# A hybrid decoder step: table load and splits placed behind the last Silu, mixer work dealt anew among ScalarE, VectorE and GpSimd

## The chip, the cores and the metric

The kernel runs on one core of one Trainium2 chip. The metric is the device time of one execution in microseconds; the time of a kernel is the median of its runs.

## The reference, cut to what matters

512 prompt tokens and 8 single-token samples (520 columns in all) pass through one layer of width 1024. The mixer has four mLSTM heads (matrix memory with exponential gates) and four retention heads of width 128; each head's output is normalised and gated. Then come an output projection, cross-attention into 256 memory tokens, a SwiGLU feed-forward of width 2816, and a last norm. Everything is in float32.

```
def layer(x, ...):
    u = rmsnorm(x, g_mix) @ w_in
    qk, conv_new = short_conv(u[..., :2 * M], conv_buf, w_conv, b_conv)      # silu(conv)
    hm, C, n, m = mlstm_scan(mq, mk, mv, ig, lf, C0, n0, m0)                 # 4 heads, chunks of 128
    hm = head_rmsnorm(hm, g_mhead) * jax.nn.sigmoid(mo)
    rq = rope(r[..., :R]...); rk = rope(r[..., R:2 * R]...) * (R_HEAD_DIM ** -0.5)
    hr, S = retention_scan(rq, rk, rv, S0)                                   # 4 heads, chunks of 128
    hr = head_rmsnorm(hr, g_rhead) * jax.nn.silu(rg)
    x = x + jnp.concatenate([hm, hr], axis=-1) @ w_out
    x = x + cross_attn(rmsnorm(x, g_xattn), mk_mem, mv_mem, w_cq, w_co)
    hf = rmsnorm(x, g_ffn)
    x = x + (jax.nn.silu(hf @ w_gate) * (hf @ w_up)) @ w_down
    return x, conv_new, C, n, m, S

def head_rmsnorm(h, g):
    h = h * lax.rsqrt(jnp.mean(h * h, axis=-1, keepdims=True) + EPS)
    return h.reshape(B, T, H * D) * g
```

The outputs are `rmsnorm` of the result with `g_final`, the new memory keys and values, and the new states.

## The kernel before

Activations lie transposed: features on 128 partitions, the 520 columns along the free axis, in halves of 260. A float32 matrix is split into a high part in fp32r and a low remainder, and a product is made of three: high by high, high by low, low by high. A projection of 128 output columns is therefore 8 blocks of depth x 3 products x 2 halves, 48 matmuls (`proj`, `mm_k`). Weights come by DMA on SyncE's queue into `wraw`; `wload` casts them on ScalarE to `whi` and forms the remainder `wlo` on VectorE, or on GpSimd where the weight's index stands in `LO_ON_POOL`. `split` does the same for activations: the cast on ScalarE, the remainder on VectorE (`TT` in the feed-forward, `B` and `A` before).

The stages follow one another: first norm (up to 20 us), mixer (20 to 262), output projection (to 310), cross-attention (to 490), gate and up projections of the feed-forward (to 727), down projection (to 838), last output block and last norm (to 873).

In the mixer TensorE runs one projection after another: `conv_block` (`pcv`) makes q and k of a mLSTM head, `plain_block` (`ppl`) the values, `rope_block` (`prp`) q and k of a retention head, and the gate projections (`pgt`) close the stage. Between them stand the pieces of the head before, as generators that `step()` moves on: `mlstm` and `retention` fetch the samples' state (`Cs`, `Ss`, 128x1024) by a DMA on GpSimd's queue, scale it, transpose keys and values (`token_major`: `vt`, `kw`), make the decayed scores (`E`, `w`), the queries with decay (`qd`), the chunk states (`states`: `St`), the outputs (`weighted`: `hs`) and then `head_norm`. That takes the sum of squares of each of four chunks and the samples into `s5` (128x5, named `hs` in the rows), an inverse root by a seed and three Newton steps in `rsqrt_small` (`hny`, `hnt`), a scaling of `hs` by it, and five transposes `ph` on TensorE. A generator called `gates` runs beside the first head: its scans `m_r` and `b_r` on VectorE yield the decays (`pc`, `cc`, `Gb`, `ws`, `car`, `fib`).

In the feed-forward the first 4 of 22 column blocks are plain; the other 18 are made of 7 products of half matrices (`pfc`, `pfd`, `pfa`, `pfa`, `pfe`, `pfb`, `pfb`), put together in `gu`: L1230 to L1243, where a Silu of the gate half and a product give `FR`. The high and low parts of `FR`, which the down projection reads, are made by `ff_split`. The parts of the first 8 blocks stand in `A`'s place; those of blocks 8 to 21 (`unsplit`) go by `rest_split`: two after each of the last products of the last block, the others behind each second depth step of the down projection. The down projection's first two output blocks run side by side: for 8 blocks of `FR` one weight for each of the two, 96 matmuls, then the next 8 blocks.

The table preload at L1254 fetches the activation table that holds both Ln and Exp. The last output block is made in two parts of columns, of which the second is finished in two quarters: `finish` adds it to `X`, squares, and calls `rsqrt_rows` (Ln, Exp and one Newton step), then multiplies all of `X` into the output and sends it.

The order of instructions on each engine is set by a scheduler that simulates the engines, not by the order of the code; `keep_in_program_order` holds an instruction to its place in the code. Each engine then works through its own list in order, so an instruction that waits holds up all behind it on the same engine.

## Time and profile before

| | us |
|---|---|
| median of 3 runs (875.74 to 878.33) | 876.3 |
| the profiled execution | 874.8 |
| its span in the profile | 873.0 |
| TensorE busy / its weight load | 833.0 (95%) / 816.0 (93%) |
| VectorE busy | 671.6 (77%) |
| ScalarE busy | 406.7 (47%) |
| GpSimd busy | 179.4 (21%) |

PE is TensorE's matmul, PEld its weight load, DVE VectorE, ACT ScalarE, POOL GpSimd. Rows of windows give a stretch of the span (from:to), its length, the busy time of each engine with its count of instructions, TensorE's granted clock as a share of full speed, the busy share of the DMA engines and GB/s. Rows of waits give who waited for whom: the sum in us, how often, and the longest. Rows of the timeline give start and duration in us, engine, line, operation, output and inputs with their sizes, the count of instructions gathered in the row, and in brackets the idle time before it with what released it. Rows of groups give a count, the busy time and the mean in ns of one, then the idle time before them.

### The profile page before, as it was taken

What the parts mean: (1) busy time and instruction counts of PE and PEld (TensorE: products, weight loads), DVE (VectorE), ACT (ScalarE), POOL (GpSimd) and SP (SyncE); (2) the same over time, 40 slices, a digit from 0 to 9 for tenths busy, and PEclk for the clock granted to TensorE, in tenths of its full rate; (3) what the DMA queues carried; (4) which work ended last, traced back from release to release, by engine and by line L of the source; (5) the groups of instructions that cost most, each with busy time, mean ns of one, the idle gap of its engine ahead of it and who ended that gap; (6) DMA issues with size and microseconds to landing.
All of it is one profiled execution on the core that took longest, in us unless ns stands there. A gap on an engine that the chain in (4) does not pass through costs nothing.

```text
span 873.0 us, 17065 instructions
## 1 busy us (share of the span) xinstructions
PE 833.0 (95%) x6707; PEld 816.0 (93%) x6707; DVE 671.6 (77%) x1512; ACT 406.7 (47%) x798; POOL 179.4 (21%) x185
## 2 busy tenths in 40 slices
PE   6989999999999999999999899999999998999992
PEld 5989989999999999889999899999999998999992
DVE  6999999877786777876888899999999996222314
ACT  5545435434546353466442655555455555222324
POOL 5554442222024300415232400000000000000100
PEclk9999999999999999999999999999999999999996
DMA  8333223333345346894764223323334331333302
GB/s 273 99 98 124 88 94 123 124 100 125 103 147 194 114 129 200 266 305 107 241 206 149 73 73 106 111 87 110 98 98 120 117 104 59 105 96 91 107 5 98
DMA packets 32680, 110.56 MB, mean 127 GB/s; under 512 B 4000, under 2 KB 6176, under 8 KB 32344
## 3 DMA queue, kind: packets, MB, share of 16 engines
q1 hardware_dynamic: 27216, 95.80, 35.0%
q0 software_dynamic: 3616, 12.34, 4.1%
q10 hardware_dynamic: 1768, 1.34, 0.5%
q8 instruction: 53, 0.87, 0.4%
q14 instruction: 27, 0.22, 0.1%
HBM read 100.38 MB, written 9.07 MB: 125 GB/s over the span
## 4 chain that ended last, share of the span: by engine, by line
PE 73%; DVE 16%; DMA 4%; ACT 3%; issue 2%; POOL 1%; SPq 0%; DVEq 0%; ACTq 0%; POOLq 0%
PE pfd L1266 13%; PE pfb L1224 6%; PE pfa L1224 6%; PE pcq L223 5%; PE pgt L223 4%; PE pwc L223 4%; PE ppl L223 4%; PE pwo L223 3%; PE pfc L1224 3%; PE pfd L1224 3%; PE prp L223 3%; PE pfe L1224 3%; PE pfu L223 2%; DVE cv L518 2%; DVE wlo L209 2%
## 5 line engine op out<-in xcount | busy, mean ns | idle before, releaser
L208 ACT CAST whi<-wraw 128x1024 fp32r<-128x1024 f32 (+1 forms) x104 | 107.2, 1032 | 174.1 <-PE pfd L1266 66.4
L209 DVE TENSOR_TENSOR wlo<-wraw,whi 128x1024 fp32r<-128x1024 f32 (+1 forms) x85 | 110.0, 1296 | 67.2 <-ACT whi L208 65.2
L302 POOL TENSOR_TENSOR ssq<-ssq,sq 128x520 f32<-128x520 f32 x18 | 28.8, 1601 | 358.6 <-ACT sq L301 353.4
L1266 PE MATMUL pfd<-TT,whi 128*128 128x260 f32 x392 | 62.8, 283 | 0.0
L191 ACT CAST qhi<-wsum 128x512 fp32r<-128x512 f32 x72 | 42.9, 620 | 40.5 <-DVE wsum L1175 26.9
L209 POOL TENSOR_TENSOR wlo<-wraw,whi 128x1024 fp32r<-128x1024 f32 x19 | 45.6, 2398 | 66.2 <-ACT whi L208 61.2
L1224 PE MATMUL pfb<-TT,qhi 128*128 128x260 f32 x288 | 52.8, 283 | 2.4 <-DVE gu L1240 2.4
L1266 PEld LDWEIGHTS pfd<-TT,whi 128*128 128x128 f32 x392 | 53.7, 188 | 0.0
L1224 PE MATMUL pfa<-TT,qhi 128*128 128x260 f32 x288 | 53.1, 282 | 0.0
L192 DVE TENSOR_TENSOR qlo<-wsum,qhi 128x512 fp32r<-128x512 f32 x72 | 48.9, 682 | 0.6 <-ACT qhi L191 0.6
L223 PE MATMUL pwc<-B,whi 128*128 128x260 f32 x256 | 43.7, 287 | 4.2 <-DVE X L291 3.0
L223 PE MATMUL ppl<-A,whi 128*128 128x260 f32 x256 | 46.3, 294 | 0.6 <-DVE up L510 0.6
L1224 PEld LDWEIGHTS pfb<-TT,qhi 128*128 128x128 f32 x288 | 44.4, 188 | 2.6 <-ACT TT L191 2.6
L223 PE MATMUL pcv<-A,whi 128*128 128x260 f32 x256 | 45.3, 293 | 0.4 <-ACT whi L208 0.4
L1224 PEld LDWEIGHTS pfa<-TT,qhi 128*128 128x128 f32 x288 | 44.3, 188 | 0.0
L223 PE MATMUL pgt<-A,whi 128*128 128x260 f32 x256 | 44.0, 287 | 0.0
L223 PE MATMUL prp<-A,whi 128*128 128x260 f32 x256 | 43.8, 287 | 0.0
L223 PE MATMUL pcq<-A,whi 128*128 128x260 f32 x256 | 42.0, 283 | 0.0
L223 PE MATMUL pwo<-B,whi 128*128 128x260 f32 x256 | 41.4, 283 | 0.0
L1224 PE MATMUL pfb<-TT,qlo 128*128 128x260 f32 x144 | 40.7, 283 | 0.0
L223 PEld LDWEIGHTS pwc<-B,whi 128*128 128x128 f32 x256 | 35.8, 188 | 5.3 <-DVE X L291 3.7
L1224 PE MATMUL pfa<-TT,qlo 128*128 128x260 f32 x144 | 40.5, 281 | 0.0
(437 smaller groups left out, 2617.5 us busy)
## 6 DMA issues: line engine op xcount, KB each, us to landing
wraw<-in_weights_dram SPq DMA_DIRECT2D x132, 512.0 KB, 3.7
kv<-in_cache_k_dram SPq DMA_DIRECT2D x16, 512.0 KB, 4.4
kv<-in_cache_v_dram SPq DMA_DIRECT2D x16, 512.0 KB, 4.4
wraw<-in_weights_dram SPq DMA_DIRECT2D x8, 384.0 KB, 3.0
X<-in_x_dram SPq DMA_DIRECT2D x2, 1040.0 KB, 6.2
Cs<-in_state_C_dram POOLq DMA_DIRECT2D x4, 512.0 KB, 4.9
out_dram<-Cs POOLq DMA_DIRECT2D x4, 512.0 KB, 3.2
Ss<-in_state_S_dram POOLq DMA_DIRECT2D x4, 512.0 KB, 3.9
```

Source lines behind the costliest of these rows:

```text
L191: act.copy(hi, src)
L192: dve.tensor_tensor(lo, src, hi.bitcast(F32), ALU.subtract)
L208: act.copy(hi[:, :n], raw[:, :n])
L209: (pool if index in LO_ON_POOL else dve).tensor_tensor(lo[:, :n], raw[:, :n], hi[:, :n].bitcast(F32), ALU.subtract)
L223: pe.matmul(ps[:m, a, :H2], w[:, k, c0 : c0 + m], x[:, s, xk, a * H2 : (a + 1) * H2], start=first and w is hi and s == 0, stop=last and w ...
L302: (dve if ob == KB - 1 else pool).tensor_tensor(ssq, ssq, s, ALU.add)
L518: dve.scalar_tensor_tensor(cv[:, :LO], up[:, j : j + LO], wc(j), cv[:, :LO], ALU.mult, ALU.add)
L1224: pe.matmul(out, w[:, k * P : (k + 1) * P], x[:, k * H2 : (k + 1) * H2], start=k == 0 and w is wh and x is xh, stop=k == 3 and w is wl,)
L1266: pe.matmul(ps[:, a, :H2], w[:, k - k0], ff(s, k, slice(a * H2, (a + 1) * H2)), start=k == 0 and w is hi and s == 0, stop=k == FB - 1 and ...
```

## The change

It has three parts. The table preload is placed behind the last Silu of the feed-forward, by an edge of order instead of a place in the code. The splits of blocks 8 to 21 are placed behind that Silu and behind the last product into `FR` (`read`), and those from block 16 on keep their place in the code. In the mixer: three weights' remainders go from GpSimd to VectorE, as do the gating of k, the last addition of the rope, the `qd` products and the two products that scale the rope's tables; the swap of halves in the rope goes through two copies on ScalarE; the scaling of `Cs` goes from one GpSimd instruction a head to eight on ScalarE, one for each sample; in the head norms the Newton steps and the small products around them go from VectorE to GpSimd, the five scalings from VectorE to ScalarE, and there is one more `yield`.

```diff
-LO_ON_POOL = {2, 4, 11, *range(52, 56), *range(60, 72)}
+LO_ON_POOL = {*range(52, 56), *range(60, 72)}
...
-            act.copy(hi, src)
-            dve.tensor_tensor(lo, src, hi.bitcast(F32), ALU.subtract)
+            return act.copy(hi, src), dve.tensor_tensor(lo, src, hi.bitcast(F32), ALU.subtract)
...
-    def rsqrt_small(pl, v, shape, tag, steps=3):
+    def rsqrt_small(pl, v, shape, tag, steps=3, on_pool=False):
...
-        for _ in range(steps):
+        for _ in range(steps if on_pool else 0):
+            pool.tensor_tensor(t, y, y, ALU.mult)
+            pool.tensor_tensor(t, t, v, ALU.mult)
+            pool.tensor_scalar(t, t, -0.5, 1.5, ALU.mult, ALU.add)
+            pool.tensor_tensor(y, y, t, ALU.mult)
+        for _ in range(0 if on_pool else steps):
...
-            if kb < 4:
-                dve.scalar_tensor_tensor(dst[:, :T], th[:, :T], 1.0, cv[:, :T], ALU.add, ALU.mult)
-            else:
-                pool.tensor_scalar(dst[:, :T], th[:, :T], 1.0, None, ALU.add)
-                pool.tensor_tensor(dst[:, :T], dst[:, :T], cv[:, :T], ALU.mult)
+            dve.scalar_tensor_tensor(dst[:, :T], th[:, :T], 1.0, cv[:, :T], ALU.add, ALU.mult)
...
-            sw = tm("sw")[:, :N]
+            sn, sw = (tm(z)[:, :N] for z in ("sn", "sw"))
+            dve.tensor_tensor(halves(sn), ps[:, :, :H2], halves(sinr), ALU.mult)
             dve.tensor_tensor(halves(dst), ps[:, :, :H2], halves(cosr), ALU.mult)
-            dve.tensor_tensor(halves(sw[:64]), ps[64:, :, :H2], halves(sinr[64:]), ALU.mult)
-            dve.tensor_tensor(halves(sw[64:]), ps[:64, :, :H2], halves(sinr[:64]), ALU.mult)
-            pool.tensor_tensor(dst, dst, sw, ALU.add)
+            act.copy(sw[:64], sn[64:])
+            act.copy(sw[64:], sn[:64])
+            dve.tensor_tensor(dst, dst, sw, ALU.add)
...
             if rho is not None:
-                dve.tensor_tensor(s5, s5, rho, ALU.mult)
-                dve.tensor_tensor(s5, s5, rho, ALU.mult)
-            dve.tensor_scalar(s5, s5, 1.0 / HD, EPS, ALU.mult, ALU.add)
-            f5 = rsqrt_small(sm, s5, [P, 5], "hn")
+                pool.tensor_tensor(s5, s5, rho, ALU.mult)
+                pool.tensor_tensor(s5, s5, rho, ALU.mult)
+            pool.tensor_scalar(s5, s5, 1.0 / HD, EPS, ALU.mult, ALU.add)
+            f5 = rsqrt_small(sm, s5, [P, 5], "hn", on_pool=True)
             if rho is not None:
-                dve.tensor_tensor(f5, f5, rho, ALU.mult)
+                pool.tensor_tensor(f5, f5, rho, ALU.mult)
+            yield
             for j in range(TB):
-                dve.tensor_scalar(hs[:, j, :HD], hs[:, j, :HD], f5[:, j : j + 1], None, ALU.mult)
-            dve.tensor_scalar(hs[:NS, 4, :HD], hs[:NS, 4, :HD], f5[:NS, 4:5], None, ALU.mult)
+                act.activation(hs[:, j, :HD], hs[:, j, :HD], AF.Copy, scale=f5[:, j : j + 1])
+            act.activation(hs[:NS, 4, :HD], hs[:NS, 4, :HD], AF.Copy, scale=f5[:NS, 4:5])
...
-            pool.tensor_tensor(Cs, Cs, fib[:, :, 0, h].unsqueeze(2).broadcast_to([P, NS, HD]), ALU.mult)
+            for b in range(NS):
+                act.activation(Cs[:, b], Cs[:, b], AF.Copy, scale=fib[:, b, 0, h : h + 1])
...
-            pool.tensor_tensor(qd, qd, q[:, P:T].rearrange("p (c t) -> p c t", c=TB - 1), ALU.mult)
+            dve.tensor_tensor(qd, qd, q[:, P:T].rearrange("p (c t) -> p c t", c=TB - 1), ALU.mult)
...
-                pool.tensor_tensor(cosr, cosr, r_bc, ALU.mult)
-                pool.tensor_tensor(sinr, sinr, r_bc, ALU.mult)
+                dve.tensor_tensor(cosr, cosr, r_bc, ALU.mult)
+                dve.tensor_tensor(sinr, sinr, r_bc, ALU.mult)
...
-            ff_split(f, FR[:, f - KB])
+            with tc.issue_after(silu.ins), tc.issue_after(read.ins):
+                both = ff_split(f, FR[:, f - KB])
+            if f >= 2 * KB:
+                for ins in both:
+                    tc.keep_in_program_order(ins)
...
-                act.activation(g2, g2, AF.Silu)
+                silu = act.activation(g2, g2, AF.Silu)
                 to = FR[:, f - KB if f >= KB else f]
-                dve.tensor_tensor(halves(to), gu[:, 0:2], gu[:, 2:4], ALU.mult)
+                read = dve.tensor_tensor(halves(to), gu[:, 0:2], gu[:, 2:4], ALU.mult)
...
-                if j > 3:
-                    rest_split(2)
...
-    tc.keep_in_program_order(act.preload_act_table_set(LOG_EXP))
+    with tc.issue_after(silu.ins):
+        act.preload_act_table_set(LOG_EXP)
```

ScalarE at the end of the feed-forward's last block, before (L1254 is the preload, L1233 and L1241 are Silus, `TT<-FR` are casts of splits, `whi` and `qhi` of weights):

```order
L191 CAST TT<-FR 128x520 x3
L1254 ACT_TABLE_LOAD
L191 CAST TT<-FR 128x520
L191 CAST qhi<-wsum 128x512
L191 CAST TT<-FR 128x520
L208 CAST whi<-wraw 128x1024
L191 CAST TT<-FR 128x520 x3
L1233 ACT_TABLE_LOAD
L1233 ACTIVATE gu<-gu 128x260
L1241 ACTIVATE gu<-gu 128x260
L191 CAST TT<-FR 128x520 x3
L1241 ACTIVATE gu<-gu 128x260
```

The same place of the changed kernel (L1260 is the preload, L1240 and L1248 are Silus):

```order
L191 CAST qhi<-wsum 128x512
L207 CAST whi<-wraw 128x1024
L1240 ACTIVATE gu<-gu 128x260
L1248 ACTIVATE gu<-gu 128x260 x2
L1260 ACT_TABLE_LOAD
L191 CAST TT<-FR 128x520 x8
L207 CAST whi<-wraw 128x1024 x2
L191 CAST TT<-FR 128x520 x4
```

The load stands behind the last Silu now, and the casts of the splits of blocks 8 to 21 behind the load; before, the list had a load ahead of these Silus and a second one for them. Behind this place the list before has six more loads, all at L273 and L275, and the list of the changed kernel none.

VectorE at the same place, before (`gu<-pf..` are the readings of TensorE's products, `TT<-FR,TT` the remainders of splits):

```order
L1238 TENSOR_TENSOR gu<-pfe,gu 128x2x260
L1232 TENSOR_TENSOR gu<-pfd,gu 128x260
L192 TENSOR_TENSOR TT<-FR,TT 128x520 x4
L192 TENSOR_TENSOR qlo<-wsum,qhi 128x512
L1240 TENSOR_TENSOR gu<-pfb,gu 128x520
L1235 TENSOR_TENSOR gu<-pfa,gu 128x260
L192 TENSOR_TENSOR TT<-FR,TT 128x520 x4
L209 TENSOR_TENSOR wlo<-wraw,whi 128x1024
L1236 TENSOR_TENSOR gu<-pfa,gu 128x260
L1243 TENSOR_TENSOR FR<-gu 128x520
```

VectorE there in the changed kernel:

```order
L1239 TENSOR_TENSOR gu<-pfd,gu 128x260
L1245 TENSOR_TENSOR gu<-pfe,gu 128x2x260
L191 TENSOR_TENSOR qlo<-wsum,qhi 128x512
L1242 TENSOR_TENSOR gu<-pfa,gu 128x260
L1247 TENSOR_TENSOR gu<-pfb,gu 128x520
L208 TENSOR_TENSOR wlo<-wraw,whi 128x1024
L1243 TENSOR_TENSOR gu<-pfa,gu 128x260
L1250 TENSOR_TENSOR FR<-gu 128x520
L1245 TENSOR_TENSOR gu<-pfe,gu 128x2x260
L1247 TENSOR_TENSOR gu<-pfb,gu 128x520
L1250 TENSOR_TENSOR FR<-gu 128x520
L191 TENSOR_TENSOR TT<-FR,TT 128x520 x8
```

The two groups of four splits ahead of the readings have gone behind the last product into `FR`.

ScalarE at the first mLSTM head, before (`Ms` is the high part of the samples' k and q, which TensorE's `kq` waits for):

```order
L586 COPY vt_353<-pvt 128x4x128
L521 ACTIVATE th<-cv 128x544
L489 ACTIVATE car<-car 128x16
L491 ACTIVATE ws<-ws 128x16
L516 ACTIVATE cv<-up,vec 128x544
L589 ACTIVATE kw<-pkt,ws 128x128 x4
L191 CAST Ms_351<-kq 8x256
L681 ACTIVATE E<-E,cc 128x128 x4
L688 ACTIVATE qd<-prow,Gb 128x128 x3
L208 CAST whi<-wraw 128x1024
```

ScalarE there in the changed kernel:

```order
L587 COPY vt_353<-pvt 128x4x128
L520 ACTIVATE cv<-up,vec 128x544
L666 ACTIVATE Cs<-Cs,fib 128x128 x8
L493 ACTIVATE car<-car 128x16
L495 ACTIVATE ws<-ws 128x16
L666 ACTIVATE Cs<-Cs,fib 128x128 x8
L191 CAST Ms_351<-kq 8x256
L684 ACTIVATE E<-E,cc 128x128 x4
L691 ACTIVATE qd<-prow,Gb 128x128 x3
L590 ACTIVATE kw<-pkt,ws 128x128 x4
L525 ACTIVATE th<-cv 128x544
L207 CAST whi<-wraw 128x1024
```

Sixteen scalings of states, those of two heads, now stand ahead of `Ms`, `E`, `qd` and `kw`, and `kw`, `th` and the weight cast have gone behind them.

GpSimd between two retention heads, before (L633 is the fill of `s5`, L541 the rope's addition):

```order
L541 TENSOR_TENSOR qr_2194<-qr_2194,sw 128x520
L633 MEMSET hs_2734 128x5
L541 TENSOR_TENSOR kr_2195<-kr_2195,sw 128x520
L751 DMA out_dram<-Ss 128x1024
L729 TENSOR_TENSOR qd<-qr_1872,cst 128x384
L725 DMA Ss<-in_state_S_dram 128x1024
```

GpSimd there in the changed kernel (the last four rows stand three times, one for each Newton step):

```order
L754 DMA out_dram<-Ss 128x1024
L728 DMA Ss<-in_state_S_dram 128x1024
L641 TENSOR_SCALAR hs_2474<-hs_2474 128x5
L262 TENSOR_TENSOR hnt<-hny 128x5
L263 TENSOR_TENSOR hnt<-hnt,hs_2474 128x5
L264 TENSOR_SCALAR hnt<-hnt 128x5
L265 TENSOR_TENSOR hny<-hny,hnt 128x5
```

The long products have gone, and a chain of 13 small instructions stands behind the two DMA issues.

## Rows read from the trace of the kernel before

**Rows 1.** Windows of the whole kernel's core: the mixer in two stretches

```profile
20.00:140.00 120.00, 114.63 (x934) 111.73 (x933) 113.38 (x297) 57.36 (x152) 53.64 (x75) 0.99 0.34 106
140.00:260.00 120.00, 119.64 (x1004) 118.37 (x1003) 97.23 (x304) 56.30 (x144) 26.96 (x26) 1.00 0.37 117
```

**Rows 2.** Waits of TensorE: us in total, times, longest

```profile
PE ph L651 <- DVE hs L645: 2.6, 4, 1.0
...
PE pc L462 <- DVE b_r L444: 1.1, 1, 1.1
```

**Rows 3.** Windows of three short stretches of the mixer

```profile
28.00:44.00 16.00, 16.00 (x137) 15.63 (x136) 15.16 (x40) 8.24 (x14) 10.44 (x22) 1.00 0.41 131
44.00:56.00 12.00, 10.35 (x74) 9.87 (x74) 11.94 (x26) 3.67 (x8) 4.13 (x5) 0.86 0.28 76
64.00:68.00 4.00, 2.58 (x20) 2.25 (x19) 3.94 (x6) 0.32 (x1) 2.22 (x4) 1.00 0.00 0
```

**Rows 4.** Timeline of TensorE at the handover to the down projection: start, duration

```profile
723.52 0.48 PE L1224 MATMUL pfb<-TT,qhi 128*128 128x260 f32 x2 [2.40 <-DVE gu L1240]
...
727.68 0.74 PE L1266 MATMUL pfd<-A,whi 128*128 128x260 f32 x4 [1.05 <-DVE gu L1236]
```

**Rows 5.** Timeline of VectorE at the handover

```profile
719.65 2.52 DVE L192 TENSOR_TENSOR TT<-FR,TT 128x520 fp32r<-128x520 f32 x4
...
722.69 0.69 DVE L1240 TENSOR_TENSOR gu<-pfb,gu 128x520 f32<-128x520 f32 x1
```

**Rows 6.** Timeline of ScalarE at the handover

```profile
726.31 1.14 ACT L191 CAST TT<-FR 128x520 fp32r<-128x520 f32 x2
...
733.51 1.05 ACT L208 CAST whi<-wraw 128x1024 fp32r<-128x1024 f32 x1 [0.38 <-PE pfd L1266]
```

**Rows 7.** Timeline of TensorE: the last matmul of the down projection

```profile
855.19 0.28 PE L1306 MATMUL pfd<-TT,wlo 128*128 128x260 f32 x1
```

**Rows 8.** Timeline of VectorE in the tail

```profile
855.59 2.46 DVE L1294 TENSOR_TENSOR FR<-X,r 128x780 f32<-128x780 f32 x3
857.97 0.48 DVE L1284 TENSOR_TENSOR X<-X,pfd 128x130 f32<-128x130 f32 x2
```

**Rows 9.** Timeline of ScalarE in the tail

```profile
850.65 1.28 ACT L273 ACT_TABLE_LOAD   x1 [2.47 <-PE pn L1288]
...
859.40 1.28 ACT L273 ACT_TABLE_LOAD   x1
...
864.39 1.28 ACT L275 ACT_TABLE_LOAD   x1
865.68 0.31 ACT L275 ACTIVATE nrml<-nrml 128x130 f32<-128x130 f32 x1
```

**Rows 10.** Timeline of VectorE in the first part of the mixer

```profile
25.26 1.78 DVE L276 TENSOR_TENSOR r_bc<-nrml 128x260 f32<-128x260 f32 x1
...
30.60 1.21 DVE L209 TENSOR_TENSOR wlo<-wraw,whi 128x1024 fp32r<-128x1024 f32 x1
...
36.76 2.37 DVE L518 SCALAR_TENSOR_TENSOR cv<-up,vec,cv 128x544 f32<-128x544 f32 x1
...
39.17 0.79 DVE L518 SCALAR_TENSOR_TENSOR cv<-up,vec,cv 128x544 f32<-128x544 f32 x1
```

**Rows 11.** Timeline of GpSimd in the first part of the mixer

```profile
36.16 2.39 POOL L209 TENSOR_TENSOR wlo<-wraw,whi 128x1024 fp32r<-128x1024 f32 x1
...
60.08 4.36 POOL L663 TENSOR_TENSOR Cs<-Cs,fib 128x1024 f32<-128x1024 f32 x2 [2.36 <-DMA Cs<-in_state_C_dram]
...
79.50 0.18 POOL L511 COPY cu<-up 128x3 f32<-128x3 f32 x1 [1.29 <-DVE up L509]
79.64 1.28 POOL L512 COPY cu<-up 128x24 f32<-128x24 f32 x1
```

**Rows 12.** Groups of GpSimd up to 285 us, by form: count, busy us, mean ns

```profile
L512 POOL COPY cu<-up 128x24 f32<-128x24 f32 x8 | 4.8, 602 | 0.0
```

**Rows 13.** Timeline of ScalarE at the first head

```profile
58.07 1.12 ACT L589 ACTIVATE kw<-pkt,ws 128x128 f32<-128x128 f32 x4
```

More of the change, by code (lines that the diff above doesn't have):

```diff
@@ L728, in retention @@
             qd = wk.tile([P, TB - 1, P], F32, tag="qd", name="qd", bufs=1)
-            pool.tensor_tensor(
+            dve.tensor_tensor(
                 qd, q[:, P:T].rearrange("p (c t) -> p c t", c=TB - 1),
@@ L1185, in ff_split @@
     def ff_split(f, raw):
-        split(ff(0, f, slice(None)), ff(1, f, slice(None)), raw)
+        return split(ff(0, f, slice(None)), ff(1, f, slice(None)), raw)
     unsplit = list(range(KB, FB))
```

## The prediction

> **What bounds the kernel now.** I read the views in this order: the windows, to see which engine is full in which stage; then TensorE's waits, to see where it is not; then the timelines of the places with waits. The time was 876.3 us in the median; the profiled execution took 874.8 us, with a span of 873.0, so I reckon against 874.8 and add 1.5 us at the end. Over the mixer TensorE is nearly full, and what stands beside it is VectorE: 113 of 120 us in the first half, 97 in the second, while ScalarE is half empty and GpSimd more so [rows 1]. TensorE's weight loads leave 8.3 + 1.6 = 9.9 us empty in these 240 us, so an edit in the mixer can give back about 10 us and no more. The waits by name are short: `ph` (the transposes behind a head norm) 2.6 us in four, `pc` (behind the scan `b_r`) 1.1 [rows 2]. The windows show more than the waits, because the queue also creeps: 137 matmuls in the 16 us from 28 to 44, or 8.56 per us, but 74 in the 12 us from 44 to 56, where the granted clock is 0.86, and 20 in the 4 us from 64 to 68 [rows 3].
>
> The feed-forward stage is full, except where it hands over to the down projection. There the last 24 `pfb` products wait 2.40 us and the first `pfd` 1.05 [rows 4], both for VectorE, which spends 2.52 us on four splits `TT` ahead of the reading `gu` that TensorE needs [rows 5], while ScalarE casts the high parts of those splits and of the first weights [rows 6].
>
> In the tail the last matmul of the down projection ends at 855.47 [rows 7], yet VectorE adds it to `X` only at 857.97, because it is still multiplying the first half of the output [rows 8]. ScalarE, which works out that half's norm, switches tables before every Ln and every Exp: six loads of 1.28 us, from 850.65 to 865.67 [rows 9].
>
> **The change part by part.**
>
> *Common table.* The preload now follows the last Silu, and the order of the changed kernel has no load behind it, so all six go. Two of them delay the first half: without them VectorE would be done with `FR` 2 x 1.28 = 2.56 us sooner, at 855.5, which is just when the last matmul ends; so the addition at 857.97 moves forward by 2.5 (its limit is the matmul at 855.47). The other four stand one behind another from 859.40 to 865.67 on the path to the last output DMA: 4 x 1.28 = 5.1. Sum **7.6 us**. What is late next is the matmul itself, so no more is to be had. One load remains behind the last Silu; its cover is the down projection. The load costs 1.28 us and the next ACTIVATE starts 0.01 us after its end [rows 9]. By the Trainium skill, ScalarE: Activation LUTs, section What ACT_TABLE_LOAD costs, a switch costs a drain of about 1.38 us on top, 2.66 us in all; by that six switches would give up to 16.0 us, but no such gap stands behind these loads, and the trace decides.
>
> *Last splits.* The eight splits that stood ahead of the readings go behind them: the waits of 2.40 and 1.05 vanish, **3.45 us**, and `pfd` starts at 727.68 - 3.45 = 724.2 [rows 4]. What could come due instead: TensorE has two weight blocks of 48 matmuls that touch only the old splits, 96 / 8.56 = 11.2 us, then needs `TT` 8 and a third weight block, at 735.4. The last Silu ends near 725.4 (the `pfb` products end at 724.2, the reading takes 0.69, the Silu about 0.4 for half the columns); load 1.28, eight casts at 0.57 and the weight cast 1.05 [rows 6] give 732.3, its low part 1.21 [rows 10] more, 733.5. Margin 1.9 us, hidden. Were ScalarE 3 us later than I reckon, it would cost 1.1.
>
> *Mixer, up to the first head (rows 3, second line).* At 8.56 per us the 74 matmuls need 8.6 us of the 12: 3.4 us lost behind `b_r`, which waits its turn on a full VectorE. Before it, four VectorE instructions are stretched beside GpSimd's work: the first is a product of 1.78 us at 25.26, the last and worst a conv step of 2.37 us against 0.79 alone [rows 10], just while GpSimd splits a weight for 2.39 [rows 11]; against the same forms alone the four lose 1.35, 1.05, 1.10 and 1.58, in all 5.1 us. The change takes GpSimd's three weight splits and the two table products away and gives VectorE, ahead of `b_r`, two splits at 1.21 [rows 10] and two products at 0.69 (the 128x520 form of rows 5): 3.8. So `b_r` comes 1.3 us sooner, which covers the wait of 1.1 for `pc`. I take **3.0** of 3.4; bounds 0 and 3.4.
>
> *Mixer, state products (rows 3, third line).* 20 matmuls where 34 fit: 1.7 us lost behind `Ms`, while GpSimd's two `Cs` products run for 4.36 us [rows 11]. On ScalarE the same becomes 16 ACTIVATEs of 128x128, at 0.28 us as for `kw` [rows 13], 4.5 us; but ScalarE runs in order, so the wait of the `Cs` products for their DMA, until 60.08 [rows 11], now holds up `Ms`, `E`, `qd`, `kw` and the next weight cast behind it. I give back 1.2: **0.5**; bounds -3.0 (all of `Ms` to `kw` late) and 1.7.
>
> *Mixer, head norms.* Of the 9.9 us some 4.9 are left, in which TensorE waits for `ph` and for VectorE's queue. After: about 3.5 us of fixed steps (squares, two seed instructions on VectorE, five scalings on ScalarE), then a chain of 13 (retention) or 16 (mLSTM) GpSimd instructions of 128x5. No row has such a one. The nearest small ones on GpSimd are the copies of 24 columns: mean 0.60, longest 1.28 [rows 11, 12]; free of others a copy of 3 columns takes about 0.18. I take 0.5 and 0.08 for the handing on: 14.5 x 0.58 + 3.5 = 11.9 us on average. The order puts between `ptn` and `ph` 66 to 126 matmuls, mean 98, that is 11.4 us. Heads below the mean wait (retention head 0, with 66, some 2 to 3 us), about 4 us in all; net gain **1.0**, bounds 0 and 4.9.
>
> *The rest* is laid at nothing: the rope's swap through ScalarE (two copies of 0.6 us a block, on an engine half empty [rows 1]), the `qd` and `km` products on VectorE (about 0.5 to 0.7 each against the longer collisions with GpSimd that go). Their cover is TensorE's lead of a whole projection, 48 matmuls; without it each would cost its own 0.5 to 1.3 us.
>
> Sum: 7.6 + 3.45 + 3.0 + 0.5 + 1.0 = 15.55; 874.8 - 15.55 = 859.25, and with 1.5 for the median **860.8 us**.
>
> **The rivals.**
>
> *The mixer gives nothing.* What VectorE loses ScalarE and the chain on GpSimd take, and only tail and handover pay: 876.3 - 11.05 = 865.3. For it: two new waits in place of old ones, and the waits by name are only 3.7 us [rows 2]. With the lower bounds it reaches 868.3.
>
> *Slower, by the Newton chain.* It decides at the price of one small GpSimd instruction. All other gains, with the 4.9 us, are 19.5 us, 2.4 a head; added to the cover of 11.4, a chain may last 13.8 us before the kernel is slower, so (13.8 - 3.5) / 14.5 = 0.71 us an instruction with its handing on, against my 0.58. The copies' mean with it is 0.68, their longest 1.36. At 1.36 the chain is 23.2 us and the wait 11.8 in each of 8 heads: 876.3 + 94 - 19.5 = 951. At 0.8 it is 15.1, and 876.3 + 30 - 19.5 = 887. The Trainium skill (SBUF — State Buffer, section Who interferes with whom) says that VectorE with two SBUF inputs and GpSimd reading SBUF lock each other out for whole instructions. That is a rule against this change: each tiny step may wait for one VectorE instruction; the conv row of 2.37 beside 2.39 agrees. Against the rival: a VectorE instruction lasts 113.4 / 297 = 0.38 us on average [rows 1], so a step that waits for one whole one costs 0.18 + 0.38 = 0.56, near what I take.
>
> *The change does not do what it says.* The third weight block comes late or the output half waits for something else: 876.3 - 4.5 - 5.1 - 2.0 = 864.7, within the first rival's times.
>
> **How the numbers follow.** Forecast, the mixer gaining between 2 and 10 us (855.3 to 863.3): 0.66. All of the empty time and some of the clock's loss back, below 855: 0.05. Mixer nothing, or tail or handover short (863.3 to 868.5): 0.18. Mixer losing more, but still faster by over 0.3%: 0.05. Within 0.3%, about what a measurement of this kernel can tell from no change: 0.02. Slower, by the chain: 0.04. So faster 0.94, same 0.02, slower 0.04. The range, from 854.5 to 868.5, takes in the bounds of the mixer's terms and leaves out about 0.15.
>
> **What would show it.** Tail: no table load behind the down projection; VectorE's addition for the last half starts right at the last matmul; the span from there to the end is 5 us shorter. Handover: no TensorE wait for `gu`, none for the third `whi` or `wlo`. Mixer: from 44 to 56 over 95 matmuls; `pc` no longer among the waits; 128x5 instructions on GpSimd at 0.4 to 0.65 us; `ph` waits of about 4 us in all, retention head 0 the longest. I would be wrong if those instructions average above 0.7, if ScalarE stands for `Cs` for over 3 us with TensorE idle behind it, or if VectorE stays as full in the first half.

## The result and the profile after

The changed kernel takes 856.4 us in the median (856.13 to 858.02, 4 runs) against 876.25 us before (875.74 to 878.33, 4 runs): a ratio of 0.977, with a 95% interval from 0.975 to 0.979. The forecast was 860.8, range 854.5 to 868.5. The profiled execution took 856.57 us with a span of 854.8, 18.2 us less than the 873.0 before. The medians are 19.8 apart, because the profiled execution of before lay 1.5 us below its median.

I cut both spans at the first instruction of a stage's tile on TensorE (first `ppl`, first `pwo`, first `pcq`, first `pfg`, first `pfc`, first `pfd` of the down projection, end of its last matmul). Each entry is the difference of two such starts, in us:

| stretch | before | after | gain | forecast |
|---|---|---|---|---|
| start to `ppl` | 28.45 | 28.98 | -0.53 | 0 |
| `ppl` to `pwo` (mixer) | 236.03 | 227.48 | 8.55 | 4.5 |
| `pwo` to `pcq` | 47.72 | 47.82 | -0.10 | 0 |
| `pcq` to `pfg` (cross-attention) | 181.16 | 182.76 | -1.60 | 0 |
| `pfg` to `pfc` | 36.90 | 37.03 | -0.13 | 0 |
| `pfc` to first `pfd` (handover) | 197.42 | 193.35 | 4.07 | 3.45 |
| down projection | 127.79 | 127.67 | 0.12 | 0 |
| tail | 17.53 | 9.71 | 7.82 | 7.6 |

Tail and handover came as reckoned. The mixer gave nearly twice what I had put down, and 1.6 us went lost in a stage that the change does not touch.

Windows after, columns as in [rows 1] and [rows 3]:

```profile
20.00:140.00 120.00, 120.00 (x1003) 118.22 (x1002) 99.52 (x275) 77.10 (x207) 26.14 (x91) 1.00 0.35 114
140.00:260.00 120.00, 119.89 (x1002) 118.29 (x1001) 83.09 (x222) 70.49 (x182) 29.38 (x95) 1.00 0.37 114
44.00:56.00 12.00, 12.00 (x103) 11.64 (x102) 11.83 (x29) 5.52 (x9) 4.59 (x10) 1.00 0.38 115
64.00:68.00 4.00, 4.00 (x36) 4.00 (x35) 2.84 (x5) 3.96 (x11) 0.56 (x4) 1.00 0.02 6
```

TensorE is now full in both halves; the creep from 44 to 56 is gone, and with it the granted clock of 0.86. VectorE has fallen from 113 to 100 us and from 97 to 83, ScalarE has taken 20 and 14 more. The waits of TensorE after, as in [rows 2], the first four and the only ones of over 0.6 us:

```profile
PE pg L349 <- ACT A L193: 7.4, 3, 5.3
PE pwc L222 <- DVE X L295: 3.0, 2, 2.7
PE pwc L222 <- DVE X L1123: 1.1, 2, 0.9
PE pq L944 <- DVE ssc L948: 1.0, 1, 1.0
```

`ph`, `pc`, and `gu` at the handover are no longer among them. The handover itself, VectorE and then ScalarE, answering to [rows 5, 6]:

```profile
717.62 0.70 DVE L1247 TENSOR_TENSOR gu<-pfb,gu 128x520 f32<-128x520 f32 x1 [0.62 <-PE pfb L1231]
718.80 0.70 DVE L1250 TENSOR_TENSOR FR<-gu 128x520 f32<-128x520 f32 x1 [0.49 <-ACT gu L1248]
720.75 4.97 DVE L191 TENSOR_TENSOR TT<-FR,TT 128x520 fp32r<-128x520 f32 x8 [1.24 <-ACT TT L191]
725.64 1.22 DVE L208 TENSOR_TENSOR wlo<-wraw,whi 128x1024 fp32r<-128x1024 f32 x1
```

```profile
718.35 0.42 ACT L1248 ACTIVATE gu<-gu 128x260 f32<-128x260 f32 x1 [3.58 <-DVE gu L1247]
718.79 1.28 ACT L1260 ACT_TABLE_LOAD   x1
720.09 4.32 ACT L191 CAST TT<-FR 128x520 fp32r<-128x520 f32 x8
724.31 1.05 ACT L207 CAST whi<-wraw 128x1024 fp32r<-128x1024 f32 x1
```

The eight splits stand behind the readings, one load behind the last Silu. The third weight block's `wlo` ends at 726.86 (725.64 + 1.22). TensorE's first `pfd` started at 717.42, and its first product with `TT` and that block is this row:

```profile
728.94 0.63 PE L1272 MATMUL pfd<-TT,whi 128*128 128x260 f32 x4
```

That is a margin of 2.1 us, where 1.9 was reckoned. ScalarE and VectorE in the tail, answering to [rows 8, 9], and TensorE's last matmul, to [rows 7]:

```profile
840.29 0.48 ACT L277 ACTIVATE nrml<-pn,vec 128x260 f32<-128x260 f32 x1 [2.48 <-PE pn L1294]
840.80 0.42 ACT L279 ACTIVATE nrml<-nrml 128x260 f32<-128x260 f32 x1
...
846.46 0.35 ACT L277 ACTIVATE nrml<-pn,vec 128x130 f32<-128x130 f32 x1
846.84 0.31 ACT L279 ACTIVATE nrml<-nrml 128x130 f32<-128x130 f32 x1
```

```profile
842.65 2.46 DVE L1300 TENSOR_TENSOR FR<-X,r 128x780 f32<-128x780 f32 x3
845.13 0.49 DVE L1290 TENSOR_TENSOR X<-X,pfd 128x130 f32<-128x130 f32 x2
```

```profile
844.81 0.28 PE L1312 MATMUL pfd<-TT,wlo 128*128 128x260 f32 x1
```

Ln and Exp follow each other with no load. VectorE adds the last half at 845.13, 0.04 us after the matmul's end at 845.09; before, that took 2.5 us.

### The profile page after: what moved, and what is told of

Same layout as the page of the kernel before. It is cut to its first block, busy times and chain, and to the rows that moved or that the text cites. A ratio compares the mean times of both kernels' runs of the same rounds, so it can differ in the third digit from the quotient of the medians.

```text
span 854.8 us, 17095 instructions
## 1 busy us (share of the span) xinstructions
PE 831.0 (97%) x6707; PEld 815.1 (95%) x6707; DVE 634.5 (74%) x1397; ACT 428.6 (50%) x879; POOL 152.4 (18%) x268
## 4 chain that ended last, share of the span: by engine, by line
PE 74%; DVE 5%; DMA 2%; issue 2%; POOL 1%; ACT 1%; DVEq 0%; POOLq 0%; ACTq 0%
PE pfd L1272 13%; PE pfb L1231 6%; PE pfa L1231 6%; PE pgt L222 5%; PE pcq L222 5%; PE pwc L222 4%; PE pfd L1231 3%; PE pfe L1231 3%; PE pfc L1231 3%; PE pwo L222 3%; PE prp L222 3%; PE pfu L222 2%; PE ppl L222 2%; PE pfg L222 2%; PE pfd L1312 1%
## 5 line engine op out<-in xcount | busy, mean ns | idle before, releaser
L208 POOL TENSOR_TENSOR wlo<-wraw,whi 128x1024 fp32r<-128x1024 f32 x16 | 38.4, 2397 | 61.5 <-ACT whi L207 56.4
L222 PE MATMUL ppl<-A,whi 128*128 128x260 f32 x256 | 44.1, 286 | 0.1
```

Of the source, the lines that this page charges most:

```text
L208: (pool if index in LO_ON_POOL else dve).tensor_tensor(lo[:, :n], raw[:, :n], hi[:, :n].bitcast(F32), ALU.subtract)
L222: pe.matmul(ps[:m, a, :H2], w[:, k, c0 : c0 + m], x[:, s, xk, a * H2 : (a + 1) * H2], start=first and w is hi and s == 0, stop=last and w ...
```

## The experiments

All stand beside runs of the kernel before on the same chip; its medians there were 877.8 (e1 to e4, e9 to e12) and 878.1 us (e5 to e8). The stretches of their profiled executions, cut as above, are what separates them, since the cross-attention alone differs by up to 3.5 us between executions of the same instructions in the same order (before and e1). The mixer is not fully steady either: before, e1 and e2 run the same order up to the end of the cross-attention, and their mixers last 236.0, 237.8 and 236.8 us; the order of the changed kernel, in three executions (changed, e9, e3), lasts 227.5 to 227.9.

| | mixer | cross-attention | handover | tail | median, ratio to before (95%) |
|---|---|---|---|---|---|
| before | 236.0 | 181.2 | 197.4 | 17.5 | |
| changed | 227.5 | 182.8 | 193.4 | 9.7 | 856.4, 0.977 (0.975 to 0.979) |
| e9, changed again | 227.6 | 182.9 | 193.3 | 9.8 | 858.2, 0.978 (0.975 to 0.980) |
| e1, table alone | 237.8 | 184.7 | 197.4 | 9.8 | 870.8, 0.993 (0.990 to 0.996) |
| e2, splits alone | 236.8 | 182.5 | 193.3 | 9.8 | 864.5, 0.985 (0.983 to 0.987) |
| e3, mixer alone | 227.9 | 184.2 | 197.4 | 17.5 | 870.0, 0.991 (0.990 to 0.993) |
| e4, head norms back | 233.9 | 184.7 | 193.3 | 9.7 | 865.7, 0.986 (0.983 to 0.989) |
| e5, first part back | 229.9 | 184.3 | 193.4 | 9.8 | 860.4, 0.978 (0.974 to 0.983) |
| e6, `Cs` back | 226.8 | 183.1 | 193.3 | 9.8 | 857.2, 0.975 (0.971 to 0.979) |
| e10, `Cs` back, again | 226.8 | 184.0 | 193.3 | 9.8 | 857.1, 0.976 (0.974 to 0.978) |
| e7, rope, `qd`, `km` back | 232.0 | 182.3 | 193.3 | 9.7 | 859.7, 0.978 (0.974 to 0.981) |
| e12, rope back | 227.3 | 183.4 | 193.3 | 9.7 | 857.6, 0.977 (0.974 to 0.981) |
| e11, Newton steps on VectorE | 242.3 | 182.3 | 193.4 | 9.8 | 871.5, 0.993 (0.990 to 0.995) |

### The three parts apart

e1, on the kernel before:

```diff
-                act.activation(g2, g2, AF.Silu)
+                silu = act.activation(g2, g2, AF.Silu)
...
-    tc.keep_in_program_order(act.preload_act_table_set(LOG_EXP))
+    with tc.issue_after(silu.ins):
+        act.preload_act_table_set(LOG_EXP)
```

> The kernel before with only the table preload placed behind the last Silu; splits and mixer as before. Its instruction order on ScalarE has no load behind the down projection's start. By the prediction's tail term: 876.3 - 7.6 = 868.7 us, and the two waits of TensorE for gu at the handover (2.4 and 1.1 us) stay or shrink a little, since one of the two loads ahead of the last Silus goes as well. Rival: the tail's gain needs the other parts too: 876.

The tail is 9.8 us, the handover 197.4: the tail's gain, 7.7 us, whole and alone. The median gained 7.0; its five runs spread from 868.4 to 874.8. TensorE's waits at the handover, in this kernel:

```profile
PE pfb L1224 <- DVE gu L1240: 3.0, 1, 3.0
```

This wait has grown from 2.4 to 3.0, while the one ahead of the first `pfd` has shrunk from 1.05 to 0.43, and the stage is as long as before: a load gone from ScalarE there brought nothing. Both waits end when VectorE is through with a reading `gu`.

e2, on the kernel before, the splits alone:

```diff
...
-            ff_split(f, FR[:, f - KB])
+            with tc.issue_after(silu.ins), tc.issue_after(read.ins):
+                both = ff_split(f, FR[:, f - KB])
+            if f >= 2 * KB:
+                for ins in both:
+                    tc.keep_in_program_order(ins)
...
-                if j > 3:
-                    rest_split(2)
...
```

> The kernel before with only the splits of blocks 8 to 21 placed behind the last Silu and the last product into FR; the preload keeps its place in the code. The order of this kernel shows the preload behind the last Silu all the same, and no load in the tail. If the trace of the changed kernel is read rightly (handover 4.2, tail 7.8): 876.3 - 12.0 = 864.3 us. If the tail needs the table's own edge: 876.3 - 3.5 = 872.8, with six loads in the tail.

864.5, with handover 193.3 and tail 9.8: both gains. The preload, left at its place in the code, is no longer drawn ahead of the last Silus, so that its own edge adds nothing once the splits have moved. The two parts of the change overlap: the tail's gain belongs to either.

e3 takes the changed kernel and undoes both:

```diff
-    with tc.issue_after(silu.ins):
-        act.preload_act_table_set(LOG_EXP)
+    tc.keep_in_program_order(act.preload_act_table_set(LOG_EXP))
...
-            with tc.issue_after(silu.ins), tc.issue_after(read.ins):
-                both = ff_split(f, FR[:, f - KB])
+            ff_split(f, FR[:, f - KB])
...
+                if j > 3:
+                    rest_split(2)
```

> The kernel before with only the mixer's part. By the prediction's sum the mixer gives 4.5: 871.8 us. By the changed kernel's trace, where the output projection starts 8.0 us sooner, it gives 8.0: 868.3, or 1.3 us less if the loss behind TensorE's long wait at the end of the cross-attention comes along.

The mixer is 227.9 us, 8.2 less than in the kernel before: the trace was read rightly, and the mixer's gain is independent of the other two parts. The 870.0 us are 0.991 of before; the ratios of e2 and e3 multiply to 0.976, against 0.977.

### The mixer's terms, each undone in the changed kernel

e4, the head norms back on VectorE:

```diff
...
-            f5 = rsqrt_small(sm, s5, [P, 5], "hn", on_pool=True)
+            f5 = rsqrt_small(sm, s5, [P, 5], "hn")
...
-            yield
             for j in range(TB):
-                act.activation(hs[:, j, :HD], hs[:, j, :HD], AF.Copy, scale=f5[:, j : j + 1])
+                dve.tensor_scalar(hs[:, j, :HD], hs[:, j, :HD], f5[:, j : j + 1], None, ALU.mult)
...
```

> The changed kernel with the head norms as before: Newton steps, small products and the five scalings on VectorE. By the prediction's term for the head norms (net 1.0): 857.4 us. Rival: the chain on GpSimd is so cheap that the norms' move gives all of the 4.9 us it could: 861.3, with waits of TensorE for ph back in the trace.

The mixer is 6.5 us longer. The rival (4.9) is nearer than the forecast's 1.0, though not with waits for `ph`; the scheduler made another order, and TensorE waits for other work of ScalarE and VectorE:

```profile
PE sc L598 <- ACT vt L587: 1.6, 2, 1.3
PE ppl L222 <- DVE qr L539: 1.5, 2, 1.0
...
PE prow L676 <- DVE kq L669: 1.0, 2, 0.6
```

e11 takes back only the Newton chain and the small products around it, and leaves the scalings on ScalarE:

```diff
...
-            f5 = rsqrt_small(sm, s5, [P, 5], "hn", on_pool=True)
+            f5 = rsqrt_small(sm, s5, [P, 5], "hn")
...
```

> The changed kernel with the Newton chain and the small products on VectorE, the five scalings still on ScalarE. With both on VectorE the mixer was 6.3 us longer. If the small instructions on VectorE are what costs (about 12 a head, each 0.2 us and more beside full queues), most of it comes back: 860 to 862 us. If it was the scalings, it stays within 2 us of the changed kernel.

871.5, and a mixer of 242.3 us, longer than the one before the change by 6.3. TensorE waits once more for the same two engines:

```profile
PE ppl L222 <- DVE kr L539: 2.6, 1, 2.6
PE sc L598 <- ACT vt L587: 2.1, 1, 2.1
PE prow L677 <- ACT vt L587: 1.6, 1, 1.6
```

The granted clock falls behind them, to a mean of 0.91 in this kernel's window from 180 to 220 us:

```profile
180.00:220.00 40.00, 37.05 (x286) 36.08 (x286) 22.65 (x79) 20.22 (x58) 2.34 (x6) 0.91 0.34 108
```

So the scalings' move does harm without the chain's, and with the scalings on ScalarE the chain's move is worth 14.9 us. The fourth case, the chain on GpSimd with the scalings on VectorE, was not run, and the extra `yield`, which e4 takes out and e11 keeps, was not undone alone; the 6.5 us of e4 can't be shared out among the three. How much of the waits comes from the new order and how much from the steps' own time on VectorE, which is short (0.16 to 0.20 us each), is not shown either.

e5, the first part back:

```diff
-LO_ON_POOL = {*range(52, 56), *range(60, 72)}
+LO_ON_POOL = {2, 4, 11, *range(52, 56), *range(60, 72)}
...
-                dve.tensor_tensor(cosr, cosr, r_bc, ALU.mult)
-                dve.tensor_tensor(sinr, sinr, r_bc, ALU.mult)
+                pool.tensor_tensor(cosr, cosr, r_bc, ALU.mult)
+                pool.tensor_tensor(sinr, sinr, r_bc, ALU.mult)
```

> The changed kernel with the three weight remainders and the two products on the rope's tables back on GpSimd. By the prediction's term for the first part of the mixer: +3.0, 859.4 us, with fewer than 85 matmuls from 44 to 56 us and the wait for pc back. Rival: the relief of VectorE by the rest is enough there: 856.4 and over 95 matmuls.

The mixer is 2.4 us longer, and the wait for `pc` is back; TensorE's waits in this kernel, and its window from 44 to 56 us:

```profile
PE pc L466 <- DVE b_r L448: 1.1, 1, 1.1
```

```profile
44.00:56.00 12.00, 10.68 (x91) 10.20 (x90) 11.94 (x27) 4.37 (x8) 2.56 (x4) 1.00 0.31 82
```

91 matmuls, between the two expectations. But the 74 of the kernel before are no firm mark. e1 runs the same mixer in the same order, and this is its window:

```profile
44.00:56.00 12.00, 10.35 (x88) 9.88 (x87) 11.94 (x23) 4.00 (x7) 3.81 (x5) 1.00 0.24 59
```

TensorE is busy for the same 10.35 us, at a granted clock of 1.00 instead of 0.86, and does 88 matmuls. So 14 of the way from 74 to 91 go with the clock, and at most 3 are relief by the rest of the change; the first part brings it from 91 to 103. `pc` starts 20.0 us behind the first `ppl` both before and in e5, and 18.8 us in the changed kernel. The median is 0.978 of before; against the changed kernel's 0.977 the total alone would not tell.

e6 and e10, `Cs` back on GpSimd:

```diff
-            for b in range(NS):
-                act.activation(Cs[:, b], Cs[:, b], AF.Copy, scale=fib[:, b, 0, h : h + 1])
+            pool.tensor_tensor(Cs, Cs, fib[:, :, 0, h].unsqueeze(2).broadcast_to([P, NS, HD]), ALU.mult)
```

> The changed kernel with the scaling of Cs back on GpSimd. By the prediction's term: +0.5, 856.9 us. Rival: the products of 4.4 us for two heads stretch VectorE's work beside them and hold up the Newton chains behind them on GpSimd's list: +1.7 or more, 858 and up, with waits for kq.

> The changed kernel with the scaling of Cs on GpSimd, in more rounds beside the changed kernel. The prediction's term for Cs says 0.5 us more than the changed kernel; the first look said about 1 us less. If moving Cs to ScalarE was worth nothing, the two are within 1 us; if the move is harmful, it is 1 to 2 us faster and the best version.

e9, the changed kernel itself on the same chip:

> The changed kernel itself, to stand on the same chip beside the next three. By its first runs 0.977 of the kernel before, some 856 to 858 us.

In e6 and e10, with `Cs` on GpSimd, the mixer is 0.7 to 0.8 us shorter than in the two profiles of the changed kernel, and no wait for `kq` comes back; the medians on one chip are 857.1 (854.9 to 857.4) and 858.2 (856.1 to 859.7), with ratios whose intervals overlap. The move of `Cs` is worth nothing, perhaps a little less; no better version is shown. GpSimd of e6 at the first head, and the window around it:

```profile
57.22 3.84 POOL L665 TENSOR_TENSOR Cs<-Cs,fib 128x1024 f32<-128x1024 f32 x2 [3.42 <-DMA Cs<-in_state_C_dram]
```

```profile
56.00:72.00 16.00, 16.00 (x137) 15.91 (x136) 15.94 (x40) 7.94 (x21) 6.29 (x8) 1.00 0.29 85
```

The two products are on GpSimd again, and TensorE loses nothing beside them: 137 matmuls in 16 us.

e7 and e12, the rest back, and the rope alone; the core of e7, beside the rope's lines that e12 shows:

```diff
+            if kb < 4:
+                dve.scalar_tensor_tensor(dst[:, :T], th[:, :T], 1.0, cv[:, :T], ALU.add, ALU.mult)
+            else:
+                pool.tensor_scalar(dst[:, :T], th[:, :T], 1.0, None, ALU.add)
+                pool.tensor_tensor(dst[:, :T], dst[:, :T], cv[:, :T], ALU.mult)
...
-            dve.tensor_tensor(qd, qd, q[:, P:T].rearrange("p (c t) -> p c t", c=TB - 1), ALU.mult)
+            pool.tensor_tensor(qd, qd, q[:, P:T].rearrange("p (c t) -> p c t", c=TB - 1), ALU.mult)
...
-            dve.tensor_tensor(dst, dst, sw, ALU.add)
+            pool.tensor_tensor(dst, dst, sw, ALU.add)
```

> The changed kernel with the gating of k, the qd products and the rope as before (GpSimd's long products; the rope's swap on VectorE). The prediction laid these moves at nothing: 856.4 us. Rival: long products on GpSimd stand ahead of the Newton chains and collide with VectorE's conv steps: 858 to 861, with waits for ph.

e12, of these only the rope:

```diff
-            sn, sw = (tm(z)[:, :N] for z in ("sn", "sw"))
-            dve.tensor_tensor(halves(sn), ps[:, :, :H2], halves(sinr), ALU.mult)
+            sw = tm("sw")[:, :N]
...
-            act.copy(sw[:64], sn[64:])
-            act.copy(sw[64:], sn[:64])
-            dve.tensor_tensor(dst, dst, sw, ALU.add)
+            dve.tensor_tensor(halves(sw[:64]), ps[64:, :, :H2], halves(sinr[64:]), ALU.mult)
+            dve.tensor_tensor(halves(sw[64:]), ps[:64, :, :H2], halves(sinr[:64]), ALU.mult)
+            pool.tensor_tensor(dst, dst, sw, ALU.add)
```

> The changed kernel with the rope alone as before (swap in VectorE's two products, addition on GpSimd). With rope, qd and km all back the mixer was 4.3 us longer, with a wait of 2.9 us for kq. If the rope's long additions on GpSimd are the cause, some 3 to 4 us come back: 860. If qd and km are, it stays within 1 us of the changed kernel. The prediction's zero for both says the same time as the changed kernel.

The rope alone changes nothing (mixer 227.3). With `qd` and `km` back as well the mixer is 4.5 us longer in the profile, while the ratio, 0.978, is hardly above the changed kernel's. Of the 4.5 us, 2.9 are one wait of TensorE for `kq`, behind `St`. This kernel's waits, and the timeline of ScalarE at that place:

```profile
PE kq L573 <- DVE St L617: 3.1, 2, 2.9
```

```profile
160.13 1.06 ACT L743 ACTIVATE Ss<-Ss 128x1024 f32<-128x1024 f32 x1 [5.75 <-DMA Ss<-in_state_S_dram]
161.09 0.25 ACT L615 COPY St<-pC 128x128 f32<-128x128 f32 x1
```

ScalarE stands idle for 5.75 us ahead of the scaling of `Ss`, until a DMA has landed, with the copy of `St` behind it in its list. That is the in-order block which the prediction feared for `Cs`, on another state. The changed kernel has the same scaling at 160.72 with no wait ahead of it: its list gives ScalarE other work until then. Which of the two moves brings that order is open.

### How much a longer chain costs

e8, the changed kernel with 12 Newton steps for 3:

```diff
-            f5 = rsqrt_small(sm, s5, [P, 5], "hn", on_pool=True)
+            f5 = rsqrt_small(sm, s5, [P, 5], "hn", steps=12, on_pool=True)
```

> The changed kernel with 12 Newton steps on GpSimd instead of 3, 36 more small instructions a head; the scheduler orders it anew and puts 111 to 197 matmuls between ptn and ph in seven heads and 12 in the last. At the 0.37 us for a step with its handing on that the changed kernel's trace shows, a chain is 17 to 20 us, hidden but for 2 to 4 us in some heads and all but 1.4 us of 17 in the last: some 16 to 25 us, 873 to 881 us. At the 0.58 of the prediction a chain is 28 to 30 us and each head waits 10 to 30: above 950. Were the chain of no weight at all: 856.4.

922.7 us (920.1 to 923.6), ratio 1.049 (1.045 to 1.053): the slower rival is real, with chains more than three times as long. The chains of 49 to 52 instructions lasted 14.0 to 22.1 us, 0.29 to 0.45 us an instruction: six of them 20 us or more, a little over what was expected, and the last two less. But the cost was 65 us, not 16 to 25. The waits by name, and two windows of this kernel:

```profile
PE ph L653 <- ACT hs L647: 38.6, 8, 12.9
...
PE pwo L222 <- ACT B L191: 4.3, 2, 3.5
```

```profile
140.00:260.00 120.00, 101.21 (x763) 96.43 (x762) 60.36 (x174) 56.15 (x151) 48.77 (x199) 0.90 0.27 85
260.00:330.00 70.00, 47.70 (x348) 45.00 (x348) 23.56 (x62) 25.85 (x69) 37.35 (x139) 0.80 0.22 73
```

All eight heads wait, for 38.6 us in all; with the 4.3 for `B` that leaves some 20 us, in windows whose mean granted clock is 0.90 and 0.80: for part of them TensorE ran at the lower of its two levels, and so paid for its idling a second time. My expectation had left both out, the waits in the gate stage and the clock.

## Why the prediction was right, and where it was off

The total came within 4.4 us, and luck had a part in it: the mixer gave 4.05 us more than its sum, and the cross-attention lost 1.6 us that no term foresaw.

**What bounds the kernel.** Right: TensorE's queue, with small losses behind VectorE. The 9.9 us of empty weight loads were the right ceiling: after, 1.78 + 1.71 = 3.5 are left, and the mixer gained 8.55, in which the clock from 44 to 56 is included.

**Common table.** 7.6 forecast, 7.82 measured; the two parts of it, 2.5 ahead of the last addition and four loads behind, are as reckoned. What I did not see is that the splits' move alone brings the same (e2). Behind the one load left, from 718.79 to 720.07, the next cast starts at 720.09. The Trainium skill (ScalarE: Activation LUTs, section What ACT_TABLE_LOAD costs) adds a drain of about 1.38 us to each switch; it shows in no row, and six times its 2.66 us would have been twice what the tail gave.

**Last splits.** 3.45 forecast, 4.07 measured. The wait for `qhi` (0.24), which I left standing, went too, because ScalarE had no splits ahead of that cast any more, and some tenths with it. The margin held: 2.1 us against 1.9.

**The mixer as a sum.** Its terms can't be checked by adding up what each costs when it is undone: 6.5 (e4), 2.4 (e5), -0.7 (e6) and 4.5 (e7) make 12.7, against 8.55 for the whole. Every such kernel is also a new order.

**Mixer, up to the first head.** 3.0 forecast; the stretch went from 74 to 103 matmuls, 3.4 us, and undone alone the part costs 2.4 (e5). The mechanism stands: `pc` comes 1.2 us sooner, where 1.3 was reckoned. The 3.4 us mix two losses, though. With the clock at 1.00 throughout, as in e1, the same order has 88 matmuls there, so some 1.6 us go with the clock and 1.8 with the wait and VectorE's queue.

**Mixer, state products.** 0.5 forecast; -0.7 or nothing by e6 and e10. Within its bounds (-3.0 to 1.7), but the cause that I read is not borne out: `Ms` was late and TensorE waited for it, yet with the same products on GpSimd e6 has 137 matmuls in the 16 us from 56 to 72. The wait in the kernel before, which [rows 2] leaves out:

```profile
PE kq L569 <- DVE Ms L192: 1.4, 1, 1.4
```

The products alone do not bring that loss, and no single part does: undone one by one (e4, e5, e6, e7, e11, e12) they leave 35 to 37 matmuls from 64 to 68. What took it away stays open.

**Mixer, head norms.** Here the term was mis-sized: net 1.0 forecast, 6.5 when the part alone is undone (e4). The step that failed is the price of one small GpSimd instruction, 0.58 us with its handing on, and with it the 4 us of `ph` waits that were taken off the gain: the trace after has no such wait among those of TensorE. GpSimd in the changed kernel, two steps alone, a stretched one, and beside it VectorE:

```profile
166.18 0.20 POOL L263 TENSOR_TENSOR hnt<-hnt,hs 128x5 f32<-128x5 f32 x1
166.47 0.20 POOL L264 TENSOR_SCALAR hnt<-hnt 128x5 f32<-128x5 f32 x1
...
166.75 1.20 POOL L265 TENSOR_TENSOR hny<-hny,hnt 128x5 f32<-128x5 f32 x1
```

```profile
166.68 1.21 DVE L208 TENSOR_TENSOR wlo<-wraw,whi 128x1024 fp32r<-128x1024 f32 x1
```

104 of the 116 such steps took 0.20 us and followed each other at 0.28. Twelve were stretched, up to 1.27 us, and each stood beside a VectorE instruction with both inputs in SBUF (`wlo`, `qd`, a conv step, a split, the rope's addition); the step at 166.75 ended within 0.1 us of the `wlo` beside it. With their handing on and the two seeds the eight chains took 42.4 us, 0.37 a step. The Trainium skill (SBUF — State Buffer, section Who interferes with whom) says that a VectorE instruction with two SBUF inputs contends with a GpSimd instruction that reads SBUF; the trace agrees, in which steps were stretched. What failed is my use of it, that each step meets a whole VectorE instruction. The copies of [rows 12] were no measure for a step either. Groups of GpSimd in the changed kernel, count, busy us and mean ns:

```profile
L265 POOL TENSOR_TENSOR hny<-hny,hnt 128x5 f32<-128x5 f32 x24 | 6.5, 270 | 1.8
...
L516 POOL COPY cu<-up 128x24 f32<-128x24 f32 x8 | 4.2, 520 | 0.3 <-issue 0.3
```

The same copies still take 0.52 us, beside Newton steps of 0.21 to 0.27. Why the copies collide more often was not tried.

The chain of retention head 0, which I had waiting for 2 to 3 us, was ready in time. TensorE's `ptn` and `ph`, and ScalarE's scalings between:

```profile
177.95 0.27 PE L763 MATMUL ptn<-cst,nv 128*8 128x128 f32 x1
186.68 0.49 PE L653 MATMUL ph<-cst,hs 128*128 128x128 f32 x3
```

```profile
183.28 1.27 ACT L647 ACTIVATE hs<-hs,hny 128x128 f32<-128x128 f32 x4
184.46 0.39 ACT L648 ACTIVATE hs<-hs,hny 8x128 f32<-8x128 f32 x1
```

6.9 us from the start of `ptn` to the end of the last scaling, against 8.7 until `ph`; by 0.58 a step it would have been 11, and the wait by the prediction's own figures 3.3 us rather than 2 to 3.

**The rest laid at nothing.** True of the rope (e12). For `qd` and `km` the profile says up to 4.5 us, the totals say less (e7); the cover, a whole projection, fails where ScalarE waits for a DMA in front of `St`.

**The rivals.** That the mixer gives nothing fell: e3. Its ground, waits by name of only 3.7 us, left out the 1.4 for `kq`, and the loss at the lower clock has no name among the waits. That the change does not do what it says fell with the tail and the handover. Slower by the chain decides, by my reckoning, at 0.71 us a step; the measured 0.37 is far on the right side. e8 shows that it is a true danger, and dearer per us of wait than I had put it.

**What no step foresaw** is the loss of 1.6 us in the cross-attention. No effect of the change shows in it: e2, whose order up to there is the one before, has 182.5 there and e1 184.7, against 181.2 in the profile of before; the changed kernel again has 182.9. The last section shows where 1.3 of the 1.6 us lie.

## What to carry to other kernels

Cut both spans at the first instruction of each stage's tile before comparing totals, and learn each stage's spread from executions of one order: here the handover repeats to 0.1 us and the tail to 0.2, the mixer of before varies by 1.8 and the cross-attention by 3.5, so that one noisy stage can hide 3 us of another. Price a small instruction on a shared engine by the share of the neighbour's work that it can collide with, not by the stretched ones in the trace. A chain on an idle engine is free as long as the full engine has other work to run in the meantime; beyond that it can cost more than the waits that it makes, as in e8, where waits of 43 us and a lower granted clock made 65.

## What the runs showed of the hardware

After the same wait of 2.7 us for `X` at the end of the cross-attention, TensorE's next instructions ran at one level or the other. TensorE of the kernel before, and of the changed kernel:

```profile
491.82 0.74 PE L223 MATMUL pwc<-B,whi 128*128 128x260 f32 x4 [2.65 <-DVE X L291]
```

```profile
484.28 1.24 PE L222 MATMUL pwc<-B,whi 128*128 128x260 f32 x4 [2.71 <-DVE X L295]
```

Four matmuls in 0.74 us there, in 1.24 here. A window of the kernel before behind that wait, and one of the changed kernel:

```profile
492.00:494.00 2.00, 2.00 (x18) 2.00 (x19) 2.00 (x4) 1.98 (x4) 0.80 (x1) 1.00 0.20 80
```

```profile
484.00:488.00 4.00, 3.72 (x20) 3.73 (x21) 2.88 (x6) 3.56 (x5) 2.27 (x2) 0.59 0.20 81
```

Granted 1.00 in the one (2.4 GHz); a mean of 0.59 from 484 to 488 in the other, that is, half of it (1.2 GHz) for most of the stretch. In all fourteen profiles, each with that wait (2.65 to 2.72 us), the 12 matmuls from there to the end of `pwc` took from 1.7 to 3.0 us, with the same code in that place: 1.7 before, 3.0 after, 1.7 in e3. These 1.3 us are most of what the cross-attention lost between the two profiles. What decides between the two is open.
